# Queries and keys of the second layer of an encoder, computed four heads at a time as token-column blocks

## The chip, the cores and the metric

The kernel runs on one core of a Trainium2 chip. The metric is device microseconds of one execution (us). Before the change the median of three runs is 878.52 us (877.7 to 879.36). The profile is of one more execution, which took 878.32 us.

## The reference

The program is a trunk of two attention layers over 256 tokens of width 2048, all in float32. `rms(x, g) = x * rsqrt(mean(x*x) + 1e-5) * g`.

```
layer 0:  proj = rms(x, ln_ab) @ w_in_ab          # 16 heads: windowed (8 query, 2 key heads) and dilated (8)
          y = attention(proj) * silu(z);  x = x + y @ w_out_ab
layer 1:  q, k, v, z = split(rms(x, ln_c) @ w_in_c, 4)   # 2048 columns each, 16 heads of 128
          per head: p = softmax(q k' / sqrt(128) + rpb table), o = p v
          x = x + (concat(o) * silu(z)) @ w_out_c
out = rms(x, ln_f)
```

The change is in layer 1, in how q and k come out of the projection.

## The kernel before

**Products.** Every float32 matrix product is made of three products: each operand is split into a rounded part (`h`) and the rest (`lo`), both of type float32r, and h·h, h·lo and lo·h are added up in PSUM. Activations lie in `xx` (and `yy`) as 16 chunks of 128 features by [h | lo] by 256 tokens. Weights come from DRAM in units of 128x1024 (`load_unit`, tile `raw`, five buffers); `split` (L142, L143) makes `wh` on ScalarE and `wl` on VectorE, three buffers each. A unit can so be split up to two units ahead of the one that TensorE is using.

**Two forms of block.** `block_tm` (token rows) makes 256 tokens by 512 columns in two PSUM banks: per chunk, for each of two groups of 128 tokens, three matmuls with a piece of `xx` as the stationary operand and 512 weight columns moving: 96 matmuls of 512 columns from 8 units. `block_fm` (feature rows) makes 128 features of one head by 256 tokens in one bank: 16 matmuls with `wh` stationary and [h | lo], 512 columns, moving, and 16 with `wl` stationary and h alone, 256 columns, moving, from 2 units. Two column halves then have to be added (`total`, L174 and L175).

**Order.** `PLAN` lists the blocks, and the main loop emits them one after the other. `tick` counts: a block of 512 columns in token form has four ticks, a feature block one, and `later(lag, f)` emits f after so many ticks. In layer 1 each group of four heads is a `v` block in token form and then k, q, k, q, k, q, k, q as feature blocks; the four gate blocks `z` and the output blocks `o` follow. A head's work is emitted in steps: at the second tick, counting its q block's own as the first, `scores` (L362 to L383: 6 matmuls, bias table, softmax), then one tick apart `transposes`, `back`, `parts` and `values` (L411: 6 matmuls).

**Turning.** `turn` transposes 32x32 blocks on VectorE into `tt` (L244) and writes them to DRAM (`bounce`, L246); `turned` reads them back in four pieces (`pT`, L253) so that the whole is transposed. The probabilities of each head go this way, the gates too. All DMAs are issued by SyncE in one queue, the weight units among them.

**Who orders the instructions.** The order above is that of the program. A list scheduler of the language decides the order on each engine, by this order and by its own estimate of when operands are ready, and adds the waits. An engine executes its own instructions in that order.

**Evacuation of q and k.** `evac_plain` (q) adds the halves and splits the sum. `evac_scaled` (k) does that and multiplies by the norm's factors along the tokens (`rb`, L423), and writes the keys in reversed order; the bias tables are reversed to match, and the probabilities are turned round again in L383.

Of the kernel before, what the change touches and what calls it, by code (L numbers as in the profile page):

```python
# [10 lines left out]
F32 = mybir.dt.float32  # L11
# [14 lines left out]
B = 32  # L26
# [7 lines left out]
ZC = 512  # L34
CUT = 1024
L2 = 1
EPS = 1e-5

ROW = 2048
# [5 lines left out]
def plan():  # L45
    p = []
    aq, ak, av = 0, AQ * HD, (AQ + AKV) * HD
    bq = av + AKV * HD
    bk, bv = bq + BH * HD, bq + 2 * BH * HD
    z = bq + 3 * BH * HD  # L50
    p.append(("v", "ab", bv, 512, 0))
    for h in range(2):
        p.append(("q", "ab", aq + h * HD, HD, h))
    p.append(("va", "ab", av, 256, 0))
    for g in range(AKV):
        p.append(("ka", "ab", ak + g * HD, HD, g))
    for h in range(2, AQ):
        if h % 2 == 0:
            p.append(("z", "ab", z + (h // 2 - 1) * ZC, ZC, h // 2 - 1))
        p.append(("q", "ab", aq + h * HD, HD, h))  # L60
    for h in range(BH):
        if h == 4:
            p.append(("v", "ab", bv + 512, 512, 1))
        p.append(("k", "ab", bk + h * HD, HD, AQ + h))
        p.append(("q", "ab", bq + h * HD, HD, AQ + h))
    p.append(("z", "ab", z + 3 * ZC, ZC, 3))
    for j in range(D // WO):
        p.append(("o", "oab", j * WO, WO, j))
    w = CH * HD
    for h in range(CH):  # L70
        if h % 4 == 0:
            p.append(("v", "c", 2 * w + h * HD, 512, h // 4))
        p.append(("k", "c", w + h * HD, HD, h))
        p.append(("q", "c", h * HD, HD, h))
    for j in range(CH * HD // ZC):
        p.append(("z", "c", 3 * w + j * ZC, ZC, j))
    for j in range(D // WO - 1):
        p.append(("o", "oc", j * WO, WO, j))
    p.append(("last", "oc", D - WO, WO, D // WO - 1))
    return p  # L80
# [22 lines left out]
def build(tc, ctx, xt, xr_in, wt, head, sink, rpb, tabs, gl_in, out):  # L103
# [133 lines left out]

        return [out_, lambda: None, in_, lambda: None, lambda: parts_(0), lambda: parts_(1)]

    def turn(srcs):  # L240

        tt = work.tile([P, NB, NT, NT, B], F32, name="tt")
        for t in range(NT):
            nc.vector.transpose(tt[:, :, :, t, :].rearrange("p b c i -> p c b i"), srcs[t])  # L244
        bounce = dram.tile([P, NB, NT * NT * B], F32, name="bounce")
        nc.sync.dma_start(bounce, tt.rearrange("p b c t i -> p b (c t i)"))  # L246
        return bounce

    def turned(bounce):
        pT = work.tile([P, NB, NT * NT * B], F32, name="pT")  # L250
        src = bounce.rearrange("(a j) b x -> b j a x", a=NB)
        for b in range(NB):
            nc.sync.dma_start(pT[b * B:(b + 1) * B], src[b])  # L253
        return pT
# [99 lines left out]
            else:  # L354
                pending.append((due, f))

    def scores(hh, q, k, v, tab, sink_col):
        pS = ps_a.tile([P, NT, S], F32, name="pS")
        s = work.tile([P, NT, S], F32, name="s", bufs=2)
        for t in range(NT):  # L360
            a = slice(t * P, (t + 1) * P)
            nc.tensor.matmul(pS[:, t, :], q[0][:, a], k[0], start=True, stop=False)  # L362
            nc.tensor.matmul(pS[:, t, :], q[0][:, a], k[1], start=False, stop=False)  # L363
            nc.tensor.matmul(pS[:, t, :], q[1][:, a], k[0], start=False, stop=True)  # L364
        for t in range(NT):
            nc.vector.scalar_tensor_tensor(s[:, t, :], pS[:, t, :], R["qs"][:, t:t + 1], tab[:, t, :],  # L366
                                           op0=OP.mult, op1=OP.add)
        nm = small.tile([P, NT], F32, name="nm")
        nc.vector.tensor_reduce(nm, s, axis=AX.X, op=OP.max, negate=True)  # L369
        if sink_col is not None:  # L370
            nc.vector.tensor_scalar(nm, nm, sink_col[0], None, op0=OP.min)
        den = small.tile([P, NT], F32, name="den")
        for t in range(NT):
            nc.scalar.activation(s[:, t, :], s[:, t, :], AF.Exp, bias=nm[:, t:t + 1], accum_out=den[:, t:t + 1])  # L374
        if sink_col is not None:
            es = small.tile([P, NT], F32, name="es")
            nc.scalar.activation(es, nm, AF.Exp, bias=sink_col[1])
            nc.vector.tensor_add(den, den, es)
        rd = small.tile([P, NT], F32, name="rd")
        nc.vector.reciprocal(rd, den)  # L380
        p = work.tile([P, NT, S], F32, name="p")
        for t in range(NT):
            nc.scalar.activation(p[:, t, ::-1], s[:, t, :], AF.Copy, scale=rd[:, t:t + 1])  # L383
        later(1, lambda: transposes(hh, p, v))

    def transposes(hh, p, v):
# [17 lines left out]
        later(1, lambda: values(hh, ph, pl, v))  # L404

    def values(hh, ph, pl, v):
        vh, vl, col = v
        pY = ps_a.tile([P, S], F32, name="pY")
        c0 = slice(col * HD, (col + 1) * HD)
        for c in range(NT):  # L410
            three(pY, vh[:, c, c0], vl[:, c, c0], ph[:, c, :], pl[:, c, :], c == 0, c == NT - 1)  # L411
        if hh in gates:
            nc.vector.tensor_mul(y[:, hh, :], pY, y[:, hh, :])
            split_y(hh)
            gates.remove(hh)
        else:
            nc.scalar.copy(y[:, hh, :], pY)
            heads.add(hh)

    def evac_scaled(ps, nm):  # L420

        f = work.tile([P, S], F32, name="kf", bufs=1)
        nc.vector.tensor_mul(f[:, ::-1], total(ps), R["rb"])  # L423
        h = qk.tile([P, S], F32R, name=nm + "h")
        lo = qk.tile([P, S], F32R, name=nm + "l")
        nc.scalar.copy(h, f)
        nc.vector.tensor_sub(lo, f, h.bitcast(F32))
        return h, lo
# [107 lines left out]
        nc.tensor.matmul(warm, ones, ones, start=True, stop=True)  # L536
    V, KA, cur, early = {}, {}, {}, []

    def start_head(lag, idx, q, mat):
        if mat == "ab" and idx < AQ:  # L540
            k, v, sc = KA[idx // 4], (*V["a"], idx // 4), (nsk[:, idx:idx + 1], sk[:, idx:idx + 1])
        else:
            k, v, sc = cur["k"], (*V["b"], idx % 4), None
        tab = table_ab(idx) if mat == "ab" else table_c(idx)
        later(lag, lambda: scores(idx, q, k, v, tab, sc))

    for n, (kind, mat, c0, ncols, idx) in enumerate(PLAN):
        if kind in ("v", "va"):
            pss = block_tm(ncols, xx, n == 0)
            if n == 0:  # L550
                vb0 = pss
                nc.sync.dma_start(sk, sink)
                for t in range(NT):
                    for c in range(0, D, CUT):
                        beside.append(lambda t=t, c=c: nc.sync.dma_start(xr[:, t, c:c + CUT], xr_in[t, :, c:c + CUT]))
                        chores.append(lambda t=t, c=c: [squares(t, d, WO, d // WO) for d in range(c, c + CUT, WO)])
                chores.appendleft(lambda: None)
                nc.vector.tensor_scalar(nsk, sk, -1.0, None, op0=OP.mult)
            elif kind == "va":
                norm_stats(D // WO)  # L560
                V["b"] = evac_v(vb0, 512)
                V["a"] = evac_v(pss, ncols)
            else:
                V["b"] = evac_v(pss, ncols)
        elif kind == "ka":
            KA[idx] = evac_scaled(block_fm(xx), "ka")
            if idx == 0:
                for i, (h, q) in enumerate(early):
                    start_head(2 + i, h, q, "ab")
        elif kind == "k":  # L570
            cur["k"] = evac_scaled(block_fm(xx), "k")
        elif kind == "q":
            q = evac_plain(block_fm(xx), "q")
            if mat == "ab" and idx < 2:
                early.append((idx, q))
            else:
                start_head(2, idx, q, mat)
        elif kind == "z":
            gate(block_tm(ncols, xx), idx)
        elif kind == "last":  # L580
            last_columns(c0, ncols, idx)
        else:
            if idx == 0 and mat == "oc":
                nc.sync.dma_start(gl, gl_in)
            residual(block_tm(ncols, yy), c0, ncols, idx)
            if mat == "oc":
                for t in range(NT):
                    nc.vector.tensor_mul(xr[:, t, c0:c0 + ncols], xr[:, t, c0:c0 + ncols], gl[:, c0:c0 + ncols])
            else:
                chores.extend(to_features(idx))  # L590
                if idx == D // WO - 1:
                    chores.append(lambda: norm_stats(D // WO))
        tick()
# [30 lines left out]
def bias_tables(rpb):  # L624
# [11 lines left out]
    dc = np.clip(c[None] - c[:, None] + NA_KW - 1, 0, 2 * NA_KW - 2)  # L636
    out = np.full((CH, S, S), NEG, np.float32)
    out[:, ok] = rpb[:, dr, dc][:, ok]
    return np.ascontiguousarray(out[:, :, ::-1].reshape(CH, NT, P, S).transpose(0, 2, 1, 3))


# [28 lines left out]
```

## Time and profile before

| | |
|---|---|
| median of 3 runs | 878.52 us (877.7 to 879.36) |
| profiled execution | 878.32 us; its span, first to last instruction, 876.5 us |
| TensorE matmul busy | 867.2 us, 99% |
| VectorE, ScalarE busy | 606.4 us (69%), 502.7 us (57%) |
| 16 DMA engines busy | 70% |
| mean granted TensorE clock | 0.998 of full speed (2.4 GHz) |
| layer 1's q, k, v stretch | about 405 to 691 us of the span |

Busy time of TensorE is the union of its matmuls' durations; they overlap, so two rates hide in it: the duration of one matmul (some 390 ns for 512 columns) and the step from one start to the next. In a timeline the step is read as the difference of two start times over the number of matmuls between them.

### The profile page before, as it was taken

The numbers are of one execution on the slowest core, as the hardware profiler recorded it, in microseconds if no ns is written. First come the engines' busy times: TensorE is split into PE (matmuls) and PEld (weight loads), VectorE is DVE, ScalarE is ACT, GpSimd is POOL, SyncE is SP. The second block draws the span as 40 slices with busy tenths as digits, with TensorE's granted clock in tenths as the row PEclk, the third lists the DMA queues.
The fourth block names the chain that finished last, engine by engine and source line by source line (L and its number), as shares of the span: only waits on it lengthen the run. The fifth ranks groups of instructions, "written<-read, shape, count | busy, mean of one in ns | idle before, by whom it ended". The sixth has DMA issues, their size and how long they took to land.

```text
span 876.5 us, 12696 instructions
## 1 busy us (share of the span) xinstructions
PE 867.2 (99%) x4474; PEld 744.4 (85%) x4474; DVE 606.4 (69%) x988; ACT 502.7 (57%) x874; POOL 0.9 (0%) x7
## 2 busy tenths in 40 slices
PE   9999999999999999999999999999999999999996
PEld 7898888888888888888888888889888888888885
DVE  7666877788767666667677667667767766676563
ACT  7646666666556555555456556556655665554452
POOL 0000000000000000000000000000000000000000
PEclk9999999999999999999999999999999999999999
DMA  9868686678766767776667657757756767877552
GB/s 349 296 221 257 219 257 211 216 265 274 225 214 217 239 218 250 259 242 208 239 194 240 234 192 234 244 177 231 233 196 224 225 214 234 276 255 235 195 172 96
DMA packets 93088, 201.16 MB, mean 229 GB/s; under 512 B 10464, under 2 KB 43232, under 8 KB 92896
## 3 DMA queue, kind: packets, MB, share of 16 engines
q1 hardware_dynamic: 93024, 200.35, 69.5%
q8 instruction: 35, 0.57, 0.3%
q14 instruction: 29, 0.24, 0.1%
HBM read 183.53 MB, written 16.78 MB: 229 GB/s over the span
## 4 chain that ended last, share of the span: by engine, by line
PE 98%; DVE 1%; DMA 1%; ACT 0%; ACTq 0%; issue 0%; DVEq 0%
PE pp L200 53%; PE pp L165 23%; PE pp L167 13%; PE pp L169 2%; PE pS L362 1%; PE pS L364 1%; PE pY L156 1%; PE pS L363 1%; PE pY L155 1%; PE pY L154 1%; PE pp L289 1%; PE pp L287 1%; PE pp L288 1%; DMA raw<-wt 1%; PE pn L536 0%; DVE wl L143 0%
## 5 line engine op out<-in xcount | busy, mean ns | idle before, releaser
L143 DVE TENSOR_TENSOR wl<-raw,wh 128x1024 fp32r<-128x1024 f32 x291 | 354.5, 1222 | 199.5 <-ACT wh L142 140.1
L142 ACT CAST wh<-raw 128x1024 fp32r<-128x1024 f32 x291 | 304.0, 1051 | 200.4 <-PE pp L200 154.8
L200 PE MATMUL pp<-wh,xx 128*128 128x512 f32 (+1 forms) x960 | 293.2, 384 | 0.0
L165 PE MATMUL pp<-xx,wh 128*128 128x512 f32 x870 | 208.8, 391 | 0.0
L200 PEld LDWEIGHTS pp<-wh,xx 128*128 128x128 f32 x960 | 178.5, 188 | 34.8 <-DVE xx L150 0.2
L165 PEld LDWEIGHTS pp<-xx,wh 128*128 128x128 f32 x870 | 161.2, 188 | 32.7
L200 PE MATMUL pp<-wl,xx 128*128 128x512 f32 (+1 forms) x480 | 183.8, 384 | 0.3 <-DVE wl L143 0.3
L200 PE MATMUL pp<-wh,yy 128*128 128x512 f32 x448 | 138.4, 389 | 0.0
L167 PEld LDWEIGHTS pp<-xx,wl 128*128 128x128 f32 x928 | 119.0, 191 | 4.5
L167 PE MATMUL pp<-xx,wl 128*128 128x256 f32 x928 | 120.4, 283 | 0.0
L200 PEld LDWEIGHTS pp<-wl,xx 128*128 128x128 f32 x480 | 90.5, 188 | 17.9 <-DVE wl L143 0.9
L200 PEld LDWEIGHTS pp<-wh,yy 128*128 128x128 f32 x448 | 84.1, 188 | 17.3
L200 PE MATMUL pp<-wl,yy 128*128 128x512 f32 x224 | 87.2, 389 | 0.0
L174 ACT COPY sum<-pp 128x256 f32<-128x256 f32 x58 | 21.5, 371 | 97.6 <-PE pp L169 97.6
L200 PEld LDWEIGHTS pp<-wl,yy 128*128 128x128 f32 x224 | 42.1, 188 | 8.8
L374 ACT ACTIVATE s<-s,nm 128x256 f32<-128x256 f32 x64 | 32.0, 501 | 9.9 <-DVE nm L369 8.4
L402 ACT CAST ph<-pT 128x256 fp32r<-128x256 f32 x64 | 23.8, 402 | 16.5 <-DMA pT<-bounce 16.5
L175 DVE TENSOR_TENSOR sum<-pp,sum 128x256 f32<-128x256 f32 x58 | 24.3, 419 | 11.5 <-ACT sum L174 11.4
L383 ACT ACTIVATE p<-s,rd 128x256 f32<-128x256 f32 x64 | 29.1, 503 | 2.3 <-DVE rd L380 2.3
L403 DVE TENSOR_TENSOR pl<-pT,ph 128x256 fp32r<-128x256 f32 x64 | 25.0, 419 | 7.5 <-ACT ph L402 6.7
L244 DVE STREAM_TRANSPOSE tt<-p 128x256 f32<-128x256 f32 x64 | 26.7, 436 | 4.8 <-ACT p L383 4.7
L366 DVE SCALAR_TENSOR_TENSOR s<-pS,qs,tab 128x256 f32<-128x256 f32 x64 | 29.1, 474 | 0.0
(117 smaller groups left out, 598.6 us busy)
## 6 DMA issues: line engine op xcount, KB each, us to landing
raw<-wt SPq DMA_DIRECT2D x295, 512.0 KB, 4.3
bounce<-tt SPq DMA_DIRECT2D x56, 256.0 KB, 2.8
pT<-bounce SPq DMA_DIRECT2D x224, 64.0 KB, 2.8
tab<-tabs SPq DMA_DIRECT2D x32, 128.0 KB, 4.9
tab<-rpb SPq DMA_DIRECT2D x16, 256.0 KB, 4.0
xr<-xr SPq DMA_DIRECT2D x4, 512.0 KB, 8.8
out<-xr SPq DMA_DIRECT2D x8, 256.0 KB, 2.4
y<-xt SPq DMA_DIRECT2D x7, 256.0 KB, 7.6
```

The costliest lines, as they stand in the source:

```text
L142: nc.scalar.copy(h, raw)
L143: nc.vector.tensor_sub(lo, raw, h.bitcast(F32))
L165: nc.tensor.matmul(ps, parts[u][0][:, c], aa[:, k], start=k == 0, stop=False)
L167: nc.tensor.matmul(ps[:, 0], parts[u][1][:, c], aa[:, k, 0], start=False, stop=False)
L175: nc.vector.tensor_add(c, ps[:, 0], c)
L200: nc.tensor.matmul(pss[t], aa[:, k, i // 2, t * P:(t + 1) * P], (h, lo, h)[i][:, c], start=k == 0 and i == 0, stop=k == NK - 1 and i == 2)
L244: nc.vector.transpose(tt[:, :, :, t, :].rearrange("p b c i -> p c b i"), srcs[t])
L366: nc.vector.scalar_tensor_tensor(s[:, t, :], pS[:, t, :], R["qs"][:, t:t + 1], tab[:, t, :], op0=OP.mult, op1=OP.add)
L374: nc.scalar.activation(s[:, t, :], s[:, t, :], AF.Exp, bias=nm[:, t:t + 1], accum_out=den[:, t:t + 1])
L383: nc.scalar.activation(p[:, t, ::-1], s[:, t, :], AF.Copy, scale=rd[:, t:t + 1])
L402: nc.scalar.copy(dh, src)
L403: nc.vector.tensor_sub(dl, src, dh.bitcast(F32))
```

## The change

Layer 1's plan per group of four heads becomes three token-form blocks: `q4`, `k4` and `v`, of 512 columns each, in that order. `project` copies the two PSUM banks of a block to SBUF on ScalarE (for k with the norm's factor, now one per partition) and turns it by pairs of heads into DRAM tiles named `pair`. `start_pair` fetches k and q of a pair (`turned`, eight reads), splits them into h and lo, and emits the two heads' scores: counting the tick that ends k4 as 1, the fetch of the first pair is emitted at tick 1, its split at 2, its scores at 3 and 6 (`PACE = 3`); for the second pair these are 7, 8, 9 and 12. `v` of the group is looked up when `values` runs. Keys are no longer reversed in layer 1, nor its tables; layer 0 keeps its feature blocks.

```diff
-    for h in range(CH):
-        if h % 4 == 0:
-            p.append(("v", "c", 2 * w + h * HD, 512, h // 4))
-        p.append(("k", "c", w + h * HD, HD, h))
-        p.append(("q", "c", h * HD, HD, h))
+    for j in range(CH // 4):
+        p.append(("q4", "c", j * 512, 512, j))
+        p.append(("k4", "c", w + j * 512, 512, j))
+        p.append(("v", "c", 2 * w + j * 512, 512, j))
...
-    def turn(srcs):
+    def turn(srcs, nm="bounce", n=3):
...
-        bounce = dram.tile([P, NB, NT * NT * B], F32, name="bounce")
+        bounce = dram.tile([P, NB, NT * NT * B], F32, name=nm, bufs=n)
...
-    def turned(bounce):
-        pT = work.tile([P, NB, NT * NT * B], F32, name="pT")
+    def turned(bounce, pool=work, nm="pT"):
+        pT = pool.tile([P, NB, NT * NT * B], F32, name=nm)
...
-            nc.scalar.activation(p[:, t, ::-1], s[:, t, :], AF.Copy, scale=rd[:, t:t + 1])
+            nc.scalar.activation(p[:, t, ::step], s[:, t, :], AF.Copy, scale=rd[:, t:t + 1])
...
+    def project(pss, scale):
+
+        evs = []
+        for t in range(NT):
+            ev = work.tile([P, WO], F32, name="sq")
+            nc.scalar.activation(ev, pss[t], AF.Copy, scale=scale[:, t:t + 1] if scale is not None else 1.0)
+            evs.append(ev)
+        return [turn([ev[:, i * S:(i + 1) * S] for ev in evs], "pair", 8) for i in range(2)]
+
+    def start_pair(lag, j, bq, bk):
+
+        got, tabs_ = {}, []
+
+        def in_():
+            for nm, b in (("k", bk), ("q", bq)):
+                got[nm] = turned(b, qk, "ka")
+            tabs_.append(table_c(j))
+
+        def parts_():
+            for nm in "kq":
+                src = got[nm].rearrange("p a (c t i) -> p c t a i", c=NT, t=NT)
+                got[nm] = []
+                for c in range(NT):
+                    h = qk.tile([P, S], F32R, name=nm + "h", bufs=3 if nm == "q" else 2)
+                    lo = qk.tile([P, S], F32R, name=nm + "l", bufs=3 if nm == "q" else 2)
+                    hv, lv = (e.rearrange("p (t a i) -> p t a i", t=NT, a=NB) for e in (h, lo))
+                    nc.scalar.copy(hv, src[:, c])
+                    nc.vector.tensor_sub(lv, src[:, c], hv.bitcast(F32))
+                    got[nm].append((h, lo))
+
+        def score(i):
+            v = (lambda: V[j // 4], j % 4 + i)
+            scores(j + i, got["q"][i], got["k"][i], v, tabs_[i], None, 1)
+
+        later(lag, in_)
+        later(lag + 1, parts_)
+        later(lag + 2, lambda: score(0))
+        later(lag + 3, lambda: tabs_.append(table_c(j + 1)))
+        later(lag + 2 + PACE, lambda: score(1))
...
+        elif kind == "q4":
+            cur["q4"] = project(block_tm(ncols, xx), None)
+        elif kind == "k4":
+            bk = project(block_tm(ncols, xx), R["r"])
+            for i in range(2):
+                start_pair(1 + 2 * PACE * i, 4 * idx + 2 * i, cur["q4"][i], bk[i])
```

## Rows read from the trace of the kernel before

**Rows 1.** The page: busy us of the engines (share), chain that ended last by engine.
```profile
PE 867.2 (99%) x4474; PEld 744.4 (85%) x4474; DVE 606.4 (69%) x988; ACT 502.7 (57%) x874; POOL 0.9 (0%) x7
...
PE 98%; DVE 1%; DMA 1%; ACT 0%; ACTq 0%; issue 0%; DVEq 0%
```
**Rows 2.** Windows: stretch, length, busy us (instructions) of each engine, clock, DMA share, GB/s.
```profile
309.00:396.50 87.50, 87.50 (x393) 72.69 (x392) 58.12 (x87) 45.93 (x67) 0.00 (x0) 1.00 0.75 249
396.50:691.40 294.90, 294.90 (x1620) 257.11 (x1619) 206.62 (x338) 170.10 (x308) 0.00 (x0) 1.00 0.66 218
691.40:780.00 88.60, 88.60 (x403) 73.80 (x402) 59.74 (x90) 48.70 (x71) 0.00 (x0) 1.00 0.73 239
```
**Rows 3.** Timeline of PE, feature blocks in layer 1: start, duration of the run, count.
```profile
654.99 3.58 PE L165 MATMUL pp<-xx,wh 128*128 128x512 f32 x15
658.41 2.08 PE L167 MATMUL pp<-xx,wl 128*128 128x256 f32 x16
660.33 0.40 PE L169 MATMUL pp<-xx,wh 128*128 128x512 f32 x1
660.56 0.28 PE L362 MATMUL pS<-kh,qh 128*128 128x256 f32 x1
```
**Rows 4.** Timeline of PE, token blocks (gates), first and last of 33 x2 rows.
```profile
737.61 0.62 PE L200 MATMUL pp<-wh,xx 128*128 128x512 f32 x2
...
743.51 0.39 PE L200 MATMUL pp<-wl,xx 128*128 128x512 f32 x1
...
759.37 0.62 PE L200 MATMUL pp<-wh,xx 128*128 128x512 f32 x2
```
**Rows 5.** Instruction groups: line, engine, operation, count, busy us, mean ns, idle before.
```profile
L174 ACT COPY sum<-pp 128x256 f32<-128x256 f32 x58 | 21.5, 371 | 97.6 <-PE pp L169 97.6
L244 DVE STREAM_TRANSPOSE tt<-s 128x256 f32<-128x256 f32 x32 | 12.3, 423 | 0.4
L402 ACT CAST ph<-pT 128x256 fp32r<-128x256 f32 x64 | 23.8, 402 | 16.5 <-DMA pT<-bounce 16.5
L175 DVE TENSOR_TENSOR sum<-pp,sum 128x256 f32<-128x256 f32 x58 | 24.3, 419 | 11.5 <-ACT sum L174 11.4
L460 ACT ACTIVATE s<-pp,rh 128x512 f32<-128x512 f32 x16 | 11.0, 689 | 7.8 <-PE pp L200 7.8
L423 DVE TENSOR_TENSOR kf<-sum,rb 128x256 f32<-128x256 f32 x26 | 10.9, 418 | 0.3
```
**Rows 6.** DMA issues: count, size of each, median us from issue to landing.
```profile
bounce<-tt SPq DMA_DIRECT2D x56, 256.0 KB, 2.8
pT<-bounce SPq DMA_DIRECT2D x224, 64.0 KB, 2.8
```
**Rows 7.** One line's instructions, L253: issue ns min/median/max; landing us min/median/max.
```profile
L253 SPq DMA_DIRECT2D pT<-bounce x224: 303/424/1839, 73.2 to 790.0; - x112
...
DMA to landing us min/median/max: 1.8/2.8/7.4
```
**Rows 8.** Waits of ACT, 397 to 780 us: in total, times, longest.
```profile
ACT wh L142 <- PE pp L200: 60.6, 40, 2.2
ACT sum L174 <- PE pp L169: 57.2, 32, 2.7
ACT ph L402 <- DMA pT<-bounce: 8.0, 5, 2.9
```
**Rows 9.** Timeline of ACT at 303 to 309 us (layer 0, gate block).
```profile
303.58 0.41 ACT L402 CAST ph<-pT 128x256 fp32r<-128x256 f32 x1 [4.02 <-DMA pT<-bounce]
...
306.03 2.93 ACT L142 CAST wh<-raw 128x1024 fp32r<-128x1024 f32 x3
```
**Rows 10.** Timeline of PE in the same stretch.
```profile
307.43 0.61 PE L200 MATMUL pp<-wh,xx 128*128 128x512 f32 x2
308.38 0.50 PE L200 MATMUL pp<-wl,xx 128*128 128x512 f32 x1 [0.33 <-DVE wl L143]
```
**Rows 11.** Timeline of DVE in the gate block of rows 4.
```profile
741.46 2.32 DVE L143 TENSOR_TENSOR wl<-raw,wh 128x1024 fp32r<-128x1024 f32 x2
```

More of the change, by code (lines that the diff above doesn't have):

```diff
@@ L36 @@
 L2 = 1
+PACE = 3
 EPS = 1e-5
@@ L355, in tick, with scores @@
                 pending.append((due, f))
-    def scores(hh, q, k, v, tab, sink_col):
+    def scores(hh, q, k, v, tab, sink_col, step):
         pS = ps_a.tile([P, NT, S], F32, name="pS")
@@ L406, in values @@
     def values(hh, ph, pl, v):
-        vh, vl, col = v
+        vh, vl = v[0]()
+        col = v[1]
         pY = ps_a.tile([P, S], F32, name="pY")
@@ L418, in values, with evac_scaled @@
             heads.add(hh)
-    def evac_scaled(ps, nm):
+    def evac_scaled(ps, h, lo):
         f = work.tile([P, S], F32, name="kf", bufs=1)
         nc.vector.tensor_mul(f[:, ::-1], total(ps), R["rb"])
-        h = qk.tile([P, S], F32R, name=nm + "h")
-        lo = qk.tile([P, S], F32R, name=nm + "l")
         nc.scalar.copy(h, f)
@@ L537, in build, with start_head @@
     V, KA, cur, early = {}, {}, {}, []
-    def start_head(lag, idx, q, mat):
-        if mat == "ab" and idx < AQ:
-            k, v, sc = KA[idx // 4], (*V["a"], idx // 4), (nsk[:, idx:idx + 1], sk[:, idx:idx + 1])
-        else:
-            k, v, sc = cur["k"], (*V["b"], idx % 4), None
-        tab = table_ab(idx) if mat == "ab" else table_c(idx)
-        later(lag, lambda: scores(idx, q, k, v, tab, sc))
+    def start_head(lag, idx, q):
+        if idx < AQ:
+            k, v, sc = KA[idx // 4], (lambda: V["a"], idx // 4), (nsk[:, idx:idx + 1], sk[:, idx:idx + 1])
+        else:
+            vb = V["b"]
+            k, v, sc = cur["k"], (lambda: vb, idx % 4), None
+        tab = table_ab(idx)
+        later(lag, lambda: scores(idx, q, k, v, tab, sc, -1))
@@ L563, in build @@
             else:
-                V["b"] = evac_v(pss, ncols)
+                V["b" if mat == "ab" else idx] = evac_v(pss, ncols)
+        elif kind == "q4":
[4 more added lines that the diff above has]
+                start_pair(1 + 2 * PACE * i, 4 * idx + 2 * i, cur["q4"][i], bk[i])
         elif kind == "ka":
-            KA[idx] = evac_scaled(block_fm(xx), "ka")
+            ka = qk.tile([P, 2, S], F32R, name="ka")
+            KA[idx] = evac_scaled(block_fm(xx), ka[:, 0, :], ka[:, 1, :])
             if idx == 0:
                 for i, (h, q) in enumerate(early):
-                    start_head(2 + i, h, q, "ab")
+                    start_head(2 + i, h, q)
         elif kind == "k":
-            cur["k"] = evac_scaled(block_fm(xx), "k")
+            ps = block_fm(xx)
+            cur["k"] = evac_scaled(ps, *(qk.tile([P, S], F32R, name="k" + e) for e in "hl"))
         elif kind == "q":
@@ L576, in build @@
             else:
-                start_head(2, idx, q, mat)
+                start_head(2, idx, q)
         elif kind == "z":
@@ L638, in bias_tables @@
     out[:, ok] = rpb[:, dr, dc][:, ok]
-    return np.ascontiguousarray(out[:, :, ::-1].reshape(CH, NT, P, S).transpose(0, 2, 1, 3))
+    return np.ascontiguousarray(out.reshape(CH, NT, P, S).transpose(0, 2, 1, 3))
 def kernel(x, ln_ab, w_in_ab, sink_a, w_out_ab, ln_c, w_in_c, rpb_c, w_out_c, ln_f):
```

## The prediction

> **What bounds the kernel.** I read the page first. TensorE is busy in matmuls for 867.2 us, 99% of the span, and the chain that ended last is TensorE for 98% [rows 1]. An engine that is always busy can still be waiting between overlapping matmuls, so I read the windows next: in the stretches of output blocks, of layer 1's q, k, v and of the gates, matmul busy time equals the length of the stretch, at the full clock (level 2.4 GHz), while VectorE has 70% and ScalarE 58% in layer 1's stretch (206.62 and 170.10 of 294.90), and the DMA engines 66% [rows 2]. Then the timelines, for the step between matmuls, which busy time hides. So only two things can change the time: how long TensorE's own stream of matmuls is, and whether something new makes it wait. Everything taken from VectorE or ScalarE as such is worth nothing.
>
> **TensorE's stream.** Per group of four heads, eight feature blocks (k and q) become two token blocks. A feature block runs from 654.99 to 660.56, where the next work starts: 5.57 us [rows 3]. In it 16 matmuls of 256 columns take 660.33 − 658.41 = 1.92 us, 120 ns a step; the 15 of 512 columns before them (658.41 − 654.99 = 3.42 us) take 228 ns a step. A token block: the rows repeat every three matmuls, 33 of them from 737.61 to 759.37, that is 32 periods or 96 matmuls, just one block, in 21.76 us; 226.7 ns a step [rows 4]. The columns are the same in both (16 x 512 + 16 x 256 = 12,288 per head and tensor, 96 x 512 = 49,152 for four), but two steps of 120 ns cost 13 ns more than one of 227. Per group: 8 x 5.57 − 2 x 21.76 = 44.56 − 43.52 = 1.04 us; four groups: **4.2 us** less. The `v` blocks, the score matmuls and the value matmuls are the same in number and shape; where they break into a stream they do so as often as before.
>
> The Trainium skill, on "TensorE: Matmul & The Clock Gate", section "Back-to-back issue gap", gives a step of N/2.4 + 2.5 ns at full clock, so a cost per matmul of 2.5 ns where the rows give 13. By it a feature block is 16 x (215.8 + 109.2) = 5.20 us and a token block 96 x 215.8 = 20.72 us, an estimate of 32 x 5.20 − 8 x 20.72 = 0.7 us for the change. It speaks against the change; the trace, 226.7 and 120 ns, does not agree with it, and the rows decide.
>
> **The other engines, in layer 1.** Removed: 32 copies of a half by ScalarE (371 ns, 11.9 us), 32 additions (419 ns, 13.4 us) and 16 scalings (418 ns, 6.7 us) by VectorE [rows 5]. Added: 16 evacuations of 128x512 on ScalarE (nearest row 689 ns, 11.0 us) and 32 transposes (423 ns, 13.5 us) on VectorE. The splits into h and lo stay in number (402 and some 420 ns each). ScalarE: −0.9 us; VectorE: −6.6 us. Both lie beside TensorE; on the path they are nothing, either way, unless they come in a lump. Turning the probabilities round goes too; its instruction stays.
>
> **DMA.** 16 turned writes of 256 KB (8 blocks, 2 pairs) and 16 x 4 reads of 64 KB are added, 8.4 MB beside the 64 MB (218 GB/s x 294.9 us) that the stretch moves: 13% more, so its DMA share goes from 0.66 to about 0.75, which is what the stretches beside it run at with TensorE never idle [rows 2]. Bias tables are fetched as before. SyncE's queue gets 64 issues of 0.42 us [rows 7], 27 us over the stretch, with the weight units behind them. ScalarE never shows a wait for a weight unit in the stretch; its casts wait for TensorE to release a buffer (60.6 us, 40 times) [rows 8], so units lie ready. I cost this at nothing; if the queue stood longer than that cover, TensorE would wait for weights.
>
> **The new wait.** A head's probabilities are written a tick before they are fetched. For the first pair of each group, the keys are fetched at the very tick that ends k4. The chain from k4's last matmul: two evacuations 1.4 us, two transposes 0.85, write 2.8 [rows 6], eight issues 3.4, landing of the last 2.8, four casts and a subtraction 2.0: 13.2 us. Its scores are emitted three ticks on, counting k4's own: two ticks of two units of 2.72 us, 10.9 us after k4. So the scheduler has to move the scores 2.3 us or more behind their place, and it does so by its own estimate of the landing. Behind the waiting cast on ScalarE's queue stand casts of weights; behind waiting scores on TensorE's, everything. The nearest rows: 54 of 64 casts of landed probabilities waited for nothing, ten waited 16.5 us together [rows 5]. The worst, 4.02 us, put the next weight casts off to 306.03 and stopped TensorE for some 0.5 us at 308 [rows 9, 10]; it is the one stop of that kind that I see outside start and end. Bounds for all eight pairs: from nothing (as 54 of 64; also a gain of at most 0.5 us if the order in layer 0 shifts and that stop goes) to 2.9 us for each group's first pair, the longest wait of this kind in layer 1 [rows 8], if no lead hides it: 11.6 us. I take 0.6 us in all, near the rows' many zeros: one stop like that at 308 us.
>
> **Sum.** The profiled execution's 878.3 (span 876.5 and 1.8 around it) − 4.2 + 0.6 = 874.7 us. The median shown is 0.2 above that execution, so **874.9 us**.
>
> **Rivals.**
> (a) *Lumps at the ends of blocks.* At a gate block's end, evacuation and transposes already put VectorE's next weight part off: the first of two is done at 741.46 + 1.16 = 742.62, and TensorE uses it at 743.51 [rows 4, 11]. 0.9 us of lead is left. The heads of the last group now fall later, and scores (two scalings, a maximum, some 1.8 us of VectorE) are emitted at the end of the first gate block and inside the second. If both lumps add up there and at some of the ends of q4 and k4, I price three stops of 0.9 us (1.8 less 0.9): 2.7 us in place of the 0.6, **877.0 us**. Against it: project has no tanh and no product, so its lump is smaller than a gate's, and VectorE has less to do in all.
> (b) *Late keys, slower.* The chain of the first pairs is late by more than the scheduler thinks, and TensorE, which takes its matmuls in order, stands at the first scores of each group. With 2.9 us at each of four groups: 878.5 − 4.2 + 11.6 = **885.9 us**. It makes the kernel slower by over 0.2% from 1.5 us per group on ((4.2 + 1.8) / 4). For it: 13.2 against 10.9 us, landings of up to 7.4 us for a median of 2.8 [rows 7], and twice as many reads in a row as a head has. Against it: the scheduler allows for landings, since most casts waited for nothing.
> (c) *The narrow matmuls are no dearer.* If the 13 ns belonged to the place in the stream and not to the width, and the token blocks kept them, equal columns would cost equal time and nothing would be gained: **878.5 us**. Against it: both steps are read in this kernel, 120 and 227 ns, in blocks of just the kind that goes and the kind that comes. The step rule of the Trainium skill, weighed above, would put the time at 877.8 us, an estimate; by the two steps of the rows it does not hold here.
> (d) *The change doesn't do what it says.* The fetch ahead is not ahead for the second pairs either; then (b) comes eight times, 897.5 us. Their writes land five ticks and more before the fetch, so I give it almost nothing.
>
> **Chances.** Forecast (873.5 to 876.2 us) 0.63; (a) 0.15, of which 0.06 still faster; (b) and (d) 0.18, of which 0.04 within the bound; (c) 0.04, no change. About 0.2% (1.8 us) is what a measurement of this kernel can tell from no change. Faster: 0.63 + 0.06 = 0.69. Same: 0.09 + 0.04 + 0.04 = 0.17. Slower: 0.14. The range goes from 873.3 us (all of the 4.2 us, the stop at 308 us gone as well, and half a us of scatter) to 879.0 us, which takes in (a), (c) and the mild end of (b); outside are nearly all of (b), 0.14, and a few hundredths of the others.
>
> **What would show it.** Right: in layer 1 only 512-wide matmuls in the projections, steps of 227 ns through q4, k4 and v, each of these 21.8 us long apart from the heads' own matmuls, the stretch about 4 us shorter, no TensorE idle time before pS. VectorE's sum some 6 to 7 us lower, DMA share of the stretch near 0.75. Wrong by (b): ScalarE waiting for the landing of a pair's fetch, or pS matmuls that start after a gap. By (a): TensorE waiting for `wl` or `wh` just behind a block's end. By (c): steps above 230 ns in q4 and k4. My forecast falls if the stretch is not shorter though TensorE shows no wait.

## The result, and the profile after

The changed kernel takes 889.49 us (median of four runs, 888.75 to 890.14) against 878.36 (four runs) for the one before: a ratio of 1.0125 (95% interval 1.0108 to 1.0143). It is slower by 11 us, where 874.9 was forecast; it lies outside the range, on the other side of no change.

First the page of the changed kernel, the lines that answer to [rows 1], and its windows over layer 1's q, k, v and over the gates, which answer to [rows 2]. The border is the start of the gates' first matmul, 688.4 here and 691.4 before.

```profile
PE 868.9 (98%) x4218; PEld 732.5 (83%) x4218; DVE 599.0 (67%) x972; ACT 502.8 (57%) x858; POOL 0.9 (0%) x7
...
PE 96%; ACT 1%; DVE 1%; DMA 1%; issue 0%; SPq 0%; ACTq 0%; DVEq 0%
```
```profile
396.10:688.40 292.30, 290.19 (x1345) 241.41 (x1344) 192.01 (x305) 163.41 (x272) 0.00 (x0) 1.00 0.71 240
688.40:792.50 104.10, 97.05 (x427) 79.29 (x426) 68.36 (x107) 56.03 (x93) 0.00 (x0) 0.97 0.70 237
```

TensorE has still 98% of the span, so the page alone hardly shows it. The windows do: the gates' stretch, from their first matmul to the first that reads `yy`, was 90.0 us long with TensorE busy throughout; it is now 104.1 us with 7 us of idle time, and its granted clock is 0.97. Of the 14.1 us, 11.9 are stops, as shown below, and 2.2 are the matmuls of three more steps of the last group's heads that now fall there. The q, k, v stretch has 2 us idle. VectorE fell by 7.4 us (606.4 to 599.0), where 6.6 were worked out, and it was worth nothing.

Next the steps in a token block of q or k, rows of the same kind as [rows 4], here 26 periods apart:

```profile
429.99 0.62 PE L200 MATMUL pp<-wh,xx 128*128 128x512 f32 x2
...
447.67 0.62 PE L200 MATMUL pp<-wh,xx 128*128 128x512 f32 x2
```

17.68 us for 78 matmuls: 226.7 ns a step, as forecast. The stream did get shorter; the stops ate it. The stretch from layer 1's norm to the first matmul that reads `yy` shows both. It lasts from 421.65 to 781.36 before and from 421.24 to 792.50 after, by the starts of these matmuls: 359.7 and 371.3 us. To split it I took every step from one matmul's start to the next that exceeds its usual length (227 ns for 512 columns, 120 for 256) by more than 25 ns, and summed the excess: 0.1 us before, 15.8 us after, 3.9 among q, k, v and 11.9 among the gates. So 11.6 = 15.7 − 4.1: the stream is 4.1 us shorter, and 15.7 us of stops are new. The gates' stops stand at three places, near 701, 738 and 755 us, with 1.8, 5.4 and 4.7 us.

The two largest, in the timeline of TensorE:

```profile
737.98 0.28 PE L156 MATMUL pY<-ph,vl 128*128 128x256 f32 x1
741.02 0.73 PE L200 MATMUL pp<-wh,xx 128*128 128x512 f32 x2 [2.77 <-ACT wh L142]
742.28 0.71 PE L200 MATMUL pp<-wl,xx 128*128 128x512 f32 x1 [0.53 <-DVE wl L143]
742.79 0.63 PE L200 MATMUL pp<-wh,xx 128*128 128x512 f32 x1
743.22 0.63 PE L200 MATMUL pp<-wl,xx 128*128 128x512 f32 x1
...
755.03 0.28 PE L156 MATMUL pY<-ph,vl 128*128 128x256 f32 x1
757.33 0.73 PE L200 MATMUL pp<-wh,xx 128*128 128x512 f32 x2 [2.02 <-ACT wh L142]
```

TensorE waits for `wh`, the split of the next weight unit. Behind the first stop the step is 0.43 us (742.79 to 743.22), about twice the usual one: the stop is paid a second time by a lower clock, 0.61 granted from 741.4 to 745.8 and 0.56 from 759.0 to 762.7, a mixture of the levels 1.2 and 2.4 GHz. The longer steps behind both stops add up to 3.0 us, which are part of the 11.9:

```profile
741.40:745.80 4.40, 3.87 (x11) 2.75 (x10) 3.75 (x5) 1.46 (x2) 0.00 (x0) 0.61 0.52 180
759.00:762.70 3.70, 3.70 (x11) 2.86 (x10) 1.80 (x2) 0.64 (x2) 0.00 (x0) 0.56 0.92 295
```

Why `wh` is late is read from ScalarE's timeline in the same place:

```profile
728.93 1.05 ACT L142 CAST wh<-raw 128x1024 fp32r<-128x1024 f32 x1 [1.67 <-PE pp L200]
729.88 0.71 ACT L449 CAST yy<-y 128x256 fp32r<-128x256 f32 x2
732.97 0.74 ACT L449 CAST yy<-y 128x256 fp32r<-128x256 f32 x2 [2.38 <-DVE y L478]
...
739.91 2.96 ACT L142 CAST wh<-raw 128x1024 fp32r<-128x1024 f32 x3
...
755.35 0.37 ACT L418 COPY y<-pY 128x256 f32<-128x256 f32 x1 [4.79 <-PE pY L156]
755.62 0.71 ACT L449 CAST yy<-y 128x256 fp32r<-128x256 f32 x2
756.23 1.99 ACT L142 CAST wh<-raw 128x1024 fp32r<-128x1024 f32 x2
```

Between 729.98 and 739.91 no weight is split: splits of `yy`, a head's exponentials and probabilities, the parts of another's landed probabilities, a gate block's evacuation and a copy of values stand in front, some of them waiting. At 755 a copy that waits 4.79 us for TensorE and two splits of `yy` stand in front of the very cast that TensorE needs next. And SyncE's queue, by its timeline, first in the kernel before and then in the change:

```profile
703.61 0.33 SPq L246 DMA_DIRECT2D bounce<-tt  x1
...
718.74 0.80 SPq L246 DMA_DIRECT2D bounce<-tt  x2
720.17 0.33 SPq L133 DMA_DIRECT2D raw<-wt  x1
720.75 3.65 SPq L253 DMA_DIRECT2D pT<-bounce  x8
724.50 13.53 SPq L133 DMA_DIRECT2D raw<-wt  x7
```
```profile
718.81 1.25 SPq L246 DMA_DIRECT2D bounce<-tt  x2
720.84 0.33 SPq L133 DMA_DIRECT2D raw<-wt  x1
721.22 0.43 SPq L253 DMA_DIRECT2D pT<-bounce  x1
723.85 0.32 SPq L246 DMA_DIRECT2D bounce<-tt  x1
724.22 6.73 SPq L253 DMA_DIRECT2D pT<-bounce  x11
731.04 1.33 SPq L133 DMA_DIRECT2D raw<-wt  x3
```

Before, the last head's write went out at 703.61, 15 us ahead of the first gate tiles. Now three writes and twelve reads of turned tiles, two gate tiles and one head's, went out in 12 us with one weight unit among them, and the last head's write follows at 737.98, just ahead of the next gate tiles. The next weight unit, issued at 731.04, is the one that TensorE lacks at 738. It landed 4.6 us later, at 735.6, about 4 us after ScalarE's turn to cast it (the casts before stood 2.72 us apart, the last at 728.93), and was cast at 739.91, another 4.3 us on. The unit that TensorE lacks at 755 went out at 751.25, behind nine reads, landed at 755.3, and was cast at 756.23. So both are seen, units late in the queue and ScalarE's order.

The stops among q, k, v are fewer. Nearly all of the 3.9 us lies at two places:

```profile
554.93 0.28 PE L362 MATMUL pS<-kh,qh 128*128 128x256 f32 x1
...
556.50 0.73 PE L200 MATMUL pp<-wh,xx 128*128 128x512 f32 x2 [0.69 <-ACT wh L142]
557.07 0.28 PE L362 MATMUL pS<-kh,qh 128*128 128x256 f32 x1
...
627.42 0.28 PE L362 MATMUL pS<-kh,qh 128*128 128x256 f32 x1
...
629.36 0.36 PE L362 MATMUL pS<-kh,qh 128*128 128x256 f32 x1 [1.06 <-DVE s L366]
```

These are the scores of the third and fourth head of groups 2 and 3. They are emitted three ticks apart, which is 17.8 us in group 1; here the scheduler has put the fourth head's 2.1 and 1.9 us behind the third's. The first pairs, whose keys the prediction took for the danger, begin their scores 13.6 to 15.5 us after k4's evacuation begins, and TensorE loses 0.3 us at them in all.

### The profile page after: what moved, and what is told of

It reads as the page before. It is cut to its first block, busy times and chain, and to the rows that moved or that the text cites. A ratio compares the mean times of both kernels' runs of the same rounds, so it can differ in the third digit from the quotient of the medians.

```text
span 887.8 us, 12304 instructions
## 1 busy us (share of the span) xinstructions
PE 868.9 (98%) x4218; PEld 732.5 (83%) x4218; DVE 599.0 (67%) x972; ACT 502.8 (57%) x858; POOL 0.9 (0%) x7
## 4 chain that ended last, share of the span: by engine, by line
PE 96%; ACT 1%; DVE 1%; DMA 1%; issue 0%; SPq 0%; ACTq 0%; DVEq 0%
PE pp L200 72%; PE pp L165 10%; PE pp L167 6%; PE pY L154 1%; PE pY L155 1%; PE pY L156 1%; PE pp L289 1%; PE pp L288 1%; PE pS L364 1%; PE pp L287 1%; PE pS L362 1%; PE pS L363 1%; PE pp L169 1%; DMA y<-xt 1%; DVE wl L143 1%; ACT wh L142 0%
## 5 line engine op out<-in xcount | busy, mean ns | idle before, releaser
L200 PE MATMUL pp<-wh,xx 128*128 128x512 f32 (+1 forms) x1472 | 455.2, 387 | 6.8 <-ACT wh L142 6.2
L200 PEld LDWEIGHTS pp<-wh,xx 128*128 128x128 f32 x1472 | 275.2, 189 | 62.1 <-ACT wh L142 7.0
L200 PE MATMUL pp<-wl,xx 128*128 128x512 f32 (+1 forms) x736 | 285.2, 388 | 1.9 <-DVE wl L143 1.9
L200 PEld LDWEIGHTS pp<-wl,xx 128*128 128x128 f32 x736 | 139.1, 189 | 31.1 <-DVE wl L143 4.5
L165 PE MATMUL pp<-xx,wh 128*128 128x512 f32 x390 | 93.7, 392 | 0.0
L165 PEld LDWEIGHTS pp<-xx,wh 128*128 128x128 f32 x390 | 72.1, 188 | 14.6
L167 PEld LDWEIGHTS pp<-xx,wl 128*128 128x128 f32 x416 | 53.3, 191 | 2.0
L167 PE MATMUL pp<-xx,wl 128*128 128x256 f32 x416 | 54.0, 283 | 0.0
L174 ACT COPY sum<-pp 128x256 f32<-128x256 f32 x26 | 9.6, 370 | 42.1 <-PE pp L169 42.1
L244 DVE STREAM_TRANSPOSE tt<-p 128x256 f32<-128x256 f32 x64 | 26.0, 432 | 7.4 <-ACT p L383 5.9
L369 DVE TENSOR_REDUCE nm<-s 128x2 f32<-128x512 f32 x32 | 21.7, 677 | 0.3
```

Source lines behind the costliest of these rows:

```text
L165: nc.tensor.matmul(ps, parts[u][0][:, c], aa[:, k], start=k == 0, stop=False)
L167: nc.tensor.matmul(ps[:, 0], parts[u][1][:, c], aa[:, k, 0], start=False, stop=False)
L200: nc.tensor.matmul(pss[t], aa[:, k, i // 2, t * P:(t + 1) * P], (h, lo, h)[i][:, c], start=k == 0 and i == 0, stop=k == NK - 1 and i == 2)
```

## The experiments

Theories at the start: **A**, the heads of the last group, whose scores now come at ticks 3 to 12 after k4, meet the gate blocks; **B**, the keys of each group's first pair come late and scores bunch; **C**, SyncE's queue carries the pairs' 16 writes and 64 reads, and weight units come late. The table gives each run's ratio to the kernel before and, from its profile, the stops among q, k, v and among the gates, and the length of the stretch from norm to `yy` as above. Stops elsewhere are not in these columns: 1.5 us at the first output block in e2, e3, e4 and e12, and in layer 0 1.4 us in e2 and e13 and some 8 us in e9 and e11. The scheduler orders all engines anew for each of these kernels, so two of them can differ in more than the edit.

| run | median us | ratio (95%) | stops q,k,v | stops gates | stretch |
|---|---|---|---|---|---|
| before | 878.36 | | 0.1 | 0.0 | 359.7 |
| the change | 889.49 | 1.0125 (1.0108 to 1.0143) | 3.9 | 11.9 | 371.3 |
| e1 last group features | 879.97 | 1.0019 (1.0010 to 1.0029) | 3.9 | 0.0 | 360.6 |
| e2 PACE 2 | 886.42 | 1.0089 (1.0074 to 1.0104) | 8.7 | 1.5 | 365.8 |
| e3 a tick later | 882.32 | 1.0042 (1.0027 to 1.0057) | 1.5 | 4.8 | 361.8 |
| e4 pairs by GpSimd | 892.00 | 1.0151 (1.0136 to 1.0166) | 11.2 | 2.8 | 369.6 |
| e5 e1 and e3 | 875.80 | 0.9971 (0.9960 to 0.9982) | 0.1 | 0.0 | 356.6 |
| e6 e5, pace 2 in group 3 | 880.89 | 1.0034 (1.0023 to 1.0045) | 5.6 | 0.0 | 362.1 |
| e7 no turning, heads 12 to 15 | 878.35 | 0.9998 (0.9989 to 1.0007) | 3.9 | 0.0 | 359.4 |
| e8 no softmax, heads 12 to 15 | 890.41 | 1.0139 (1.0126 to 1.0152) | 4.1 | 12.2 | 371.8 |
| e9 turning of 12 to 15 by GpSimd | 894.08 | 1.0176 (1.0157 to 1.0196) | 3.9 | 7.8 | 367.4 |
| e10 three tt | 887.40 | 1.0098 (1.0081 to 1.0114) | 2.6 | 9.8 | 368.0 |
| e11 e3 and e9 | 885.93 | 1.0088 (1.0072 to 1.0103) | 1.3 | 2.9 | 359.8 |
| e12 e3 and e10 | 881.36 | 1.0034 (1.0021 to 1.0047) | 0.1 | 5.6 | 361.3 |
| e13 gate weights by GpSimd | 886.48 | 1.0087 (1.0068 to 1.0106) | 3.9 | 6.8 | 366.4 |
| e14 gate weights by ScalarE | 894.52 | 1.0170 (1.0145 to 1.0195) | 3.9 | 15.4 | 374.9 |
| e15 e3 and e13 | 878.06 | 0.9990 (0.9980 to 1.0000) | 1.3 | 0.3 | 357.2 |
| e16 e3 and e14 | 891.58 | 1.0144 (1.0127 to 1.0161) | 1.8 | 14.4 | 372.1 |

**e1.** The plan's last group as before, in feature form (its keys not reversed).

```diff
+TOK = 3
...
-    for j in range(CH // 4):
+    for j in range(TOK):
         p.append(("q4", "c", j * 512, 512, j))
...
+    for h in range(4 * TOK, CH):
+        if h % 4 == 0:
+            p.append(("v", "c", 2 * w + h * HD, 512, h // 4))
+        p.append(("k", "c", w + h * HD, HD, h))
+        p.append(("q", "c", h * HD, HD, h))
```


> Heads 0 to 11 as in the changed kernel, heads 12 to 15 as feature blocks again, so that their scores end two ticks after the last block. Theory A (the last four heads' steps now fall on the ends of gate blocks, and ScalarE and VectorE put the next unit's split behind them): the stops of the gate blocks, some 11.6 us, go, and the stream is 1.0 us longer: about 879. Theory B (keys of each group's first pair come late, and scores bunch): one of four groups goes, about 889. Theory C (weight units come late because SyncE's queue carries the pairs' writes and reads): a quarter of all stops goes, about 887.

The stops among the gates are gone, all 11.9 us, and those among q, k, v are just what they were. A holds for the first, and 3.9 us belong to something else.

**e2.** `PACE = 2`.

> PACE 2 in place of 3: scores at ticks 3, 5, 7, 9 instead of 3, 6, 9, 12, and the last head's values at tick 13, the end of the second gate block, instead of 16. Theory A: the stop in the third gate block (about 4.5 us) goes, those at the ends of the first two stay: about 885. Theory B: heads bunch more, 889 to 892. Theory C: the queue carries the same in less time, 889 or slower.

The time is near what A gave, but not for its reason: the gates' stops nearly go, and q, k, v get 8.7 us. The largest stand again between the scores of two heads close together, 2.5 to 3.1 us apart (544.04 and 546.65, 618.70 and 621.21, 692.80 and 695.94).

**e3.** `start_pair(2 + 2 * PACE * i, ...)` in place of 1.

> Fetch, split and scores of all pairs one tick later. Theory B: the first pair's chain of 13.2 us then fits before its scores (16.3 us), the stops at scores among the q, k, v blocks (some 3.8 us) go: about 885.5. Theory A: the stops among gate blocks move by a tick and stay in size or get worse: 887 to 892 for that part alone. Theory C: no change, 889.

The stops among q, k, v fall from 3.9 to 1.5 us, as B had it, but hardly by the first pairs' keys, which had cost 0.3 us. With one tick more the scores of groups 1 and 2 stay 17 to 18 us apart throughout, and what is left lies in group 4 at 678.39 and 680.24, two scores 1.9 us apart. That the gates' stops fell too, to 4.8, A had not expected: one tick decides what meets what.

**e4.** In `turn` and `turned`, `nc.gpsimd` issues for `pair` and `ka`.

> The pairs' 16 writes and 64 reads are issued by GpSimd, which is idle, instead of SyncE. Theory C: weight units come as early as before, and the stops where ScalarE waits for a unit (around 555, 703 and 757 us) go: 884 or less. Theories A and B: the stops stay, 889, give or take 2 for another landing time of the reads.

Slower, and it shows what late keys look like. The landing of the reads rose from 2.2 to 4.6 us, and TensorE now stands at the scores themselves. The DMA row of the reads in e4, and TensorE's largest wait in layer 1:

```profile
ka<-pair POOLq DMA_DIRECT2D x64, 64.0 KB, 4.6
```
```profile
PE pS L362 <- ACT qh L573: 6.9, 4, 2.6
```

This is rival (b) of the prediction, with four waits of up to 2.6 us, one at each group's first pair. In the change itself it is not there: TensorE's waits for the same stretch name `wh`, `wl` and once the score buffer.

```profile
PE pp L200 <- ACT wh L142: 6.2, 4, 2.8
PE pp L200 <- DVE wl L143: 1.9, 4, 0.5
PE pS L362 <- DVE s L366: 1.1, 1, 1.1
```

Among the gates e4 has 2.8 us of stops, not 11.9. C would have that, but the last group's heads also come at other times in it, so it does not tell the two apart.

**e5.** The edits of e1 and e3 together.

> Heads 0 to 11 in token form with fetch, split and scores one tick later, heads 12 to 15 as feature blocks: the two edits that each took stops away, together. Theories A and B together: no stops among the gates, about 1 us or less among q, k, v, the stream 3.1 us shorter: 875 to 876, faster than the kernel before by 0.2% or more. If the stops are made by something else, they come back: 879 or more.

875.80 us: no stop is left (0.1 us, as before), and the stretch is 3.1 us shorter, three groups at 1.0. It is faster than both kernels, 0.3% faster than the one before. Its windows have TensorE busy from end to end:

```profile
422.30:690.40 268.10, 268.10 (x1322) 227.34 (x1321) 182.16 (x283) 157.54 (x281) 0.00 (x0) 1.00 0.71 242
690.40:778.90 88.50, 88.50 (x403) 73.71 (x402) 59.67 (x86) 48.93 (x72) 0.00 (x0) 1.00 0.72 245
```

**e6.** As e5, with a pace of 2 for the third group.

> As the run before it, with the third group's heads two ticks apart instead of three, so that they are out of the way of the last group's feature blocks. Theory B: less bunching, as fast as the run before it or up to 1 us faster. If bunching of scores within a group costs (as with a pace of 2 throughout), 1 to 2 us slower.

5.6 us of stops, all at 620 to 628 us, in that group: bunching within a group is what costs, as in e2, and here more than the 1 to 2 us expected. Three heads' scores come at 619.17, 621.10 and 624.92. So it is in all these runs: every stop of 0.4 us or more among q, k, v, but for e4's, stands at or just behind two scores that are 1.8 to 3.9 us apart, and no two so close go without one.

**What in the last heads does it?** A names a place, not a mechanism. In e7, e8 and e9 the test `hh >= 12` catches layer 0's heads 12 to 15 too, so I read only the columns of layer 1, not the medians.

**e7.** Turning left out for these heads: `values` multiplies probabilities that are not transposed.

```diff
-        later(1, lambda: transposes(hh, p, v))
+        if hh >= 12:
+            later(3, lambda: parts(hh, p.rearrange("p t s -> p (t s)").rearrange("p (a x) -> p a x", a=NB), v))
+        else:
+            later(1, lambda: transposes(hh, p, v))
```


> The changed kernel, but the probabilities of heads 12 to 15 are not turned: their two transposes, one write and four reads are left out, and the later steps stay at their ticks. Theory A1 (SyncE's queue: in the gate blocks the weight units stand behind these writes and reads): the stops among the gates, 11.9 us, fall to 2 or less, 879 to 880. Theory A2 (ScalarE's and VectorE's own work, in order): 8 us or more of them stay, 886 or more.

**e8.** Softmax left out: scores, clamped from below by the table, go straight to the turning. They lie in the buffers of `p`, so these heads leave those of `s`, which the gates use too.

```diff
-        s = work.tile([P, NT, S], F32, name="s", bufs=2)
+        s = work.tile([P, NT, S], F32, name="p" if hh >= 12 else "s", bufs=2)
...
-                                           op0=OP.mult, op1=OP.add)
+                                           op0=OP.mult, op1=OP.max if hh >= 12 else OP.add)
+        if hh >= 12:
+            later(1, lambda: transposes(hh, s, v))
+            return
```


> The changed kernel, but heads 12 to 15 have no softmax: maximum, exponentials, reciprocal and scaling are left out (some 2.4 us of ScalarE and 0.9 of VectorE per head), the turning stays. Theory A2: the stops among the gates fall to 4 us or less, 881 or less. Theory A1: 8 us or more of them stay, 886 or more.

The two tell it apart: without the softmax, some 3 us less engine work per head, 12.2 us of stops stay, most of them at the same two places (near 739 and 753 us); without the turning none do. SyncE's queue in e7, at the same gate block as above, is that of the kernel before again: two writes, one unit, eight reads, and then seven units in a row. But the turning is more than queue places: two transposes on VectorE, a `tt` buffer of two, a `pT` buffer of two, and landings.

**e9.** `turn` and `turned` of these heads issued by GpSimd.

> The changed kernel; the writes and reads that turn the probabilities of heads 12 to 15 are issued by GpSimd, not SyncE; all else is done as before. Turning was what the stops among the gates hung on. Theory Q (SyncE's queue: weight units behind writes that wait for a transpose, and behind reads): the stops among the gates, 11.9 us, fall to 3 or less, 881 or less. Theory T (the two tt buffers, or VectorE's transposes): they stay at 8 or more, 886 or more.

It settles less than it should. The stop at the end of the second gate block does go, but with landings of 4.8 us ScalarE waits up to 5.8 us for probabilities, layer 0 included. Of the 7.8 us of stops, 6.1 follow such a wait in the first gate block and 1.7 stay in the third.

**e10.** `tt` with three buffers.

> The changed kernel with three tt buffers instead of two (and three instead of four of the small vectors, to make room). Theory T: the gates' and the heads' transposes no longer wait for each other's write, the stops among the gates fall to 5 us or less, 883 or less. Theory Q: 9 us or more of them stay, 887 or more.

9.8 us of the gates' stops stay, so the `tt` buffers are not the main cause. **e11** and **e12** repeat e9 and e10 one tick later:

> All four groups in token form, one tick later, and the turning of heads 12 to 15 issued by GpSimd. Theory Q with B: the stops among q, k, v stay at 1.5 us, those among the gates fall from 4.8 to 1 or less, so 877 to 878; the stream is 4.2 us shorter than in the kernel before. Theory T: 882, as with one tick later alone.

> All four groups in token form, one tick later, with three tt buffers. Theory T: the stops among the gates fall to 1 us or less and those among q, k, v below 1.5, 876 to 878. Theory Q: 881 to 883, as with one tick later alone.

e12 agrees with the queue theory (5.6 us of stops among the gates against 4.8 without the buffer); e11's gates fall to 2.9, and its total is spoilt by layer 0.

**e13.** The turns stay in SyncE's queue, and the gate blocks' 32 weight units leave it; Z0 is their first unit.

```diff
-        nc.sync.dma_start(raw, wt[pos[0]])
+        (nc.gpsimd if Z0 <= pos[0] < Z0 + 32 else nc.sync).dma_start(raw, wt[pos[0]])
```


> The changed kernel; the 32 weight units of layer 1's gate blocks are issued by GpSimd, so that they no longer stand behind the writes and reads of turned tiles in SyncE's queue. Theory Q (the queue's order makes units late): the stops among the gates, 11.9 us, fall to 2 or less, 880 or less. Theory V (VectorE's transposes, or tt buffers, make the splits late): 8 us or more of them stay, 886 or more.

Neither expectation: 6.8 us stay, of 11.9. Units are no longer late (ScalarE waits 0.7 us for one in all, 3.8 before), but now it waits for landed probabilities. These two waits of ScalarE, 690 to 800 us, in e13 and then in the change:

```profile
ACT ph L403 <- DMA pT<-bounce: 15.8, 4, 6.7
...
ACT wh L143 <- DMA raw<-wt: 0.7, 1, 0.7
```
```profile
ACT wh L142 <- DMA raw<-wt: 3.8, 5, 2.0
...
ACT ph L402 <- DMA pT<-bounce: 0.7, 1, 0.7
```

**e14** and **e16** have ScalarE issue the units, **e15** has GpSimd do it one tick later.

> The same with ScalarE as the issuer, whose landings should be like SyncE's, but whose queue also holds waiting casts. Theory Q: the stops among the gates fall to 4 us or less, 882 or less. Theory V: 8 us or more stay, 886 or more.

> All four groups in token form, one tick later, gate weights issued by GpSimd. Theory Q with B: stops among q, k, v 1.5 us, among the gates 1 or less: 876 to 877, against 882.3 for one tick later alone. Theory V: 881 or more.

> As the run before it, with ScalarE issuing the gate weights. Theory Q with B: 876 to 879. Theory V: 881 or more.

With ScalarE as issuer the stops are 15.4 and 14.4 us, and it waits 20.8 and 19.5 us for units, though these land as fast (4.6 us) as by SyncE: its queue holds waiting casts, and the issues wait with them. e15's profile, of its fastest execution, has 0.3 us of stops among the gates and 1.3 among q, k, v with all four groups in token form, but its runs scatter from 875.7 to 878.9 us and their median is at the edge of no change; e5 is the better version.

So: that the gates' stops need the last four heads' turning beside the gates' own is shown (e1, e7), and so is that neither these heads' softmax work nor the `tt` buffers are the main cause (e8, e10). That weight units late in SyncE's queue are one part of it is shown by e13 and e15 against the change and e3 (11.9 to 6.8, 4.8 to 0.3; ScalarE's waits for units 3.8 to 0.7, 4.4 to none). What the other part is, stays open: casts of landed probabilities that wait in ScalarE's queue are the likeliest, since these lead its waits in e13, but no run took them away alone. A rival that no run tests are the two `pT` buffers, which heads and gates share: among the gates of the change, reads in SyncE's queue stand 3.4 us until VectorE is done with one, and the kernel before has no such wait there. For the stops among q, k, v it is shown where they come, at two heads' scores close together; why the scheduler puts them so is open.

## Why the prediction was wrong

**The stream: right.** 4.2 us were worked out. The stretch's change less its stops is −4.0 to −4.1 us for the change, e3, e7 and e15, and −3.0 to −3.1 for the three groups of e1 and e5. Rival (c), equal columns at equal time, is refuted. The step rule of the Trainium skill (page "TensorE: Matmul & The Clock Gate", section "Back-to-back issue gap"), by which, as an estimate, 0.7 us would have gone, is given there for an isolated matmul; the prediction took it for a stream, and for this stream it does not hold.

**The other engines: right where it matters.** 420 ns for a transpose (L244) where 423 was taken, 687 and 598 ns for the two evacuations (L552, for k and for q) where 689 was, and nothing gained by any of it. ScalarE's sum came out 0.1 us higher (502.8 for 502.7) where 0.9 less was worked out.

**The step that failed** is "I take 0.6 us in all" for the new wait: 15.7 us were measured, more than the 11.6 us that stood there as the upper bound. It failed in two ways.

First, the bound looked at one wait, late keys at the first pairs. These keys came somewhat later than worked out (13.6 to 15.5 us to the first scores, for 13.2), and the scheduler made room for them: 0.3 us of stops. TensorE stands at them, as (b) had it, only with landings of 4.6 us (e4). Nearly all of the 3.9 us among q, k, v came at the second pairs, for which the sum took nothing, where the scheduler put two heads' scores 2 us apart and TensorE stood at the score buffer or at weights whose casts stood behind the heads' work. They fall when the pairs come a tick later (e3) and vanish in e5.

Second, the larger part, 11.9 us, lies in the gate blocks, where rival (a) was. It named the place and the cause, the last group's heads falling later, and its sign came, TensorE waiting for `wh` just behind a block's end, at 738; the stop at 755 is inside a block. It priced three stops of 0.9 us from the lead left in one block [rows 4, 11]. That price was the wrong term: it added VectorE's instructions, and took each engine's work to be the only thing that is put off. Without the maximum and ScalarE's softmax work the stops stay (e8). What meets is the turning, 3 writes and 12 reads in one queue with the weight units, and ScalarE's order around it, and the stops that grew so long cost 3.0 us more at the lower clock. The sentence "I cost this at nothing" on SyncE's queue was made for the added 64 reads in the q, k, v stretch. There it held well enough, with 1.8 us of waits of ScalarE for units, none of them in front of a stop; but the heads' old DMAs, moved by the change into the gate blocks, were not counted there.

The DMA share of layer 1's stretch is 0.71, not 0.75.

## What to carry to other kernels

Where one engine is busy to 99% and everything else is hidden by a schedule, a change that shortens its stream by 0.5% also moves other work in time, and the move is to be costed first: list every step that falls into another stage, its DMAs above all, and what they stand in front of in each queue there. A rival that names the right place should be priced by all that meets there, not by one engine's instructions. Here 0.3% is gained by keeping the last group as it was and emitting the others one tick later (e5).

## What the runs showed of the hardware

Issued by GpSimd, reads of 64 KB landed in 4.6 to 4.8 us (e4, e9, e11) where SyncE's took 2.2 to 3.2, for transfers of the same form; weight units of 512 KB took 5.2 us in e13 and 4.7 in e15, against SyncE's 4.5 and 4.6. Where the stop of 2.8 us came, TensorE's granted clock fell to 0.61 in the stretch of 4.4 us that followed, with steps of 0.43 us.
